# A token mixer's front on one core: query products ahead of the kv/value projection, the first projection in accumulator banks, two token mixes side by side

## The chip, the core and the metric

The kernel runs on one core of a Trainium2 chip. The metric is device time in microseconds (us), from a launch of the whole program: two layers for 384 tokens. TensorE (PE) does the matmuls and transposes, VectorE (DVE), ScalarE (ACT) and GpSimd (POOL) the elementwise work, and SyncE (SP) issues the DMAs that bring weights.

## The reference

Each layer is FFN 1, token mixer, FFN 2, all with a norm ahead and one behind. The tokens are 256 of a new stream (the prompt) and 8 × 16 of running streams with a cache (the sample). The widths are 1024 for the model, 8 heads with 64 + 32 columns, 384 for the query latent (cq), 256 for the kv latent, 256 for each of the other three branches. The mixer, to which the change belongs:

```python
def token_mixer(n, cos, sin, p, cache_lat, cache_kr, buf_b, buf_d):
    b, t, _ = n.shape
    h = n @ p['w_in']
    cq, ckv, kr, glu_in, uv, dproj, g = jnp.split(h, [O_Q, O_KV, O_KR, O_B, O_C, O_D], axis=-1)

    q = (rmsnorm(cq, p['q_norm']) @ p['w_uq']).reshape(b, t, A_HEADS, NOPE_DIM + ROPE_DIM)
    q_nope = q[..., :NOPE_DIM]
    q_rope = apply_rope(q[..., NOPE_DIM:], cos[:, None], sin[:, None])
    latent = rmsnorm(ckv, p['kv_norm'])
    k_rope = apply_rope(kr, cos, sin)
    if cache_lat is None:
        a = mla_prompt(q_nope, q_rope, latent, k_rope, p['w_ukv'])
    else:
        a = mla_sample(q_nope, q_rope,
                       jnp.concatenate([cache_lat.astype(latent.dtype), latent], axis=1),
                       jnp.concatenate([cache_kr.astype(k_rope.dtype), k_rope], axis=1),
                       p['w_ukv'])

    ga, gg = jnp.split(glu_in, 2, axis=-1)
    xb = ga * jax.nn.sigmoid(gg)
    bpad = jnp.concatenate([buf_b.astype(xb.dtype), xb], axis=1)
    yb = causal_dwconv(bpad, p['conv_b_w']) + p['conv_b_bias']
    yb = jax.nn.silu(layernorm(yb, p['conv_b_ln_g'], p['conv_b_ln_b']))
    new_b = bpad[:, -(CONV_B_WIDTH - 1):]

    u, v = jnp.split(uv, 2, axis=-1)
    v = layernorm(v, p['gmlp_vn_g'], p['gmlp_vn_b'])
    if cache_lat is None:
        yc = u * spatial_mix_prompt(v, p['gmlp_w_s'], p['gmlp_b_s'])
    else:
        yc = u * spatial_mix_sample(v, p['gmlp_w_s'], p['gmlp_b_s'])

    bg, cg, hd = jnp.split(dproj, 3, axis=-1)
    xd = cg * hd
    dpad = jnp.concatenate([buf_d.astype(xd.dtype), xd], axis=1)
    yd = bg * causal_dwconv(dpad, p['conv_d_w'])
    new_d = dpad[:, -(CONV_D_WIDTH - 1):]

    gates = jax.nn.sigmoid(g).reshape(b, t, N_BRANCH, D_MODEL)
    merged = (gates[:, :, 0] * (a @ p['w_br_a']) + gates[:, :, 1] * (yb @ p['w_br_b'])
              + gates[:, :, 2] * (yc @ p['w_br_c']) + gates[:, :, 3] * (yd @ p['w_br_d']))
    return merged @ p['w_o'], (latent, k_rope, new_b, v, new_d)
```

## The kernel before

The 384 tokens lie in three tiles t = 0, 1, 2 of 128; the third is the sample. Products are in fp32r, each as three: high × high, low × high, high × low (`mm3`, L313). For a weight the high part `wh` is a cast on ACT and the low part `wl` a subtraction on DVE (`split_unit`, L246); for the normalized activations `xh` and `xl` are made likewise, out of an accumulator bank into which PE has transposed them (`chain`, L397: `flip` L431 transposes and casts, `low` L441 subtracts). All instructions are recorded by one helper, so each row of the profile says L74, and the names tell them apart.

PSUM has eight banks. Six are accumulators, `acc(t,h)` for tile t and half h (L340); `bank()` (L336) goes round the six. Two rotate (`rot`, L344).

Weights come in units, in an order that `plan_mixer` (L562) writes down. In the front of the mixer these are: four units mA (the columns for cq and the rotated key kr, 416 wide, two of eight k-rows each), two units for conv(0), four units mB (kv latent and gMLP values, 512 wide), three units uq (query products: one for the rotated part, two for the rest), two units for conv(1), two units ukv, and so on. SP loads each unit to one of four stage buffers (`load_unit`, L225), then ACT and DVE split it.

The order of instructions on each engine is fixed when the program is built. `Core` is a planner: it keeps a clock of its own, costs each instruction, holds follow-up work as generators (`spawn`, `step`, L147 to L187) and takes up the one that is due; `take` and `drop` (L163, L174) say when a bank is free. Where it thinks DVE idle, it puts a tap of the long convolution there (`tap` L699, tile yTb; 62 a layer).

In `mixer_front` (L646) the work goes: for each tile the mA product by `heads` (L376), that is, sixteen matmuls on xh and, last, eight on xl; behind each, `latent_q` (L867) takes statistics (ACT's junk), rotates the key (kr), scales cq (half) and transposes it; then conv(0); then the mB product for each tile, followed by `latent_kv` and `gmlp_v` (L901, L926); then the query products, `rotate` (L955; three tiles, each evicted as four pieces of 32 partitions, by ACT and DVE in turn) and `nope` (L984; four); then conv(1). Later `dense` (L837) hands out the projections and token mixes that fill PE during the attention: short(0), short(1), mix(0), short_gate(0), mix(1), short_gate(1) and on. The piece of `heads` on which the first step rests:

```python
                mm(o, lhsT=self.xh[:, k, tt], rhs=wh, start=(k == 0), stop=False)
                mm(o, lhsT=self.xh[:, k, tt], rhs=wl, start=False, stop=False)
...
            self.need(("xL", t))
            for k in range(KD):
                if not first:
                    mm(o, lhsT=self.xl[:, k, tt], rhs=w(k)[0], start=False, stop=(k == KD - 1))
```

Of the kernel before, what the change touches and what calls it, by code (L numbers as in the profile page):

```python
# [8 lines left out]
F32 = mybir.dt.float32  # L9
# [3 lines left out]
ALU = mybir.AluOpType  # L13
# [3 lines left out]
P = 128  # L17
D = 1024
KD = D // P
T = 384  # L20
NT = 3
DFF = 2816
NC_FF = DFF // P
EPS = 1e-6
# [9 lines left out]
KL = 256  # L34
# [14 lines left out]
PE, ACT, DVE, POOL = "tensor", "scalar", "vector", "gpsimd"  # L49
# [50 lines left out]
class Core:  # L100
# [461 lines left out]
    def plan_mixer(self, units, l):  # L562
        a = self.a
        def fm(cs):
            for c in cs:
                units.append((("fm", l, c), a["in_f"][l, c], [KD, P], "M"))

        for h in range(4):
            units.append((("mA", l, h), a["in_a"][l, :, 2 * h:2 * h + 2, :], [2, 416], "M"))
        fm(range(0, 2))  # L570
        for h in range(4):
            units.append((("mB", l, h), a["in_b"][l, :, 2 * h:2 * h + 2, :], [2, 512], "M"))
        for h in range(3):
            units.append((("uq", l, h), a["w_uq"][l, h], [3, 256], "M"))
        fm(range(2, 4))
        for h in range(2):
            units.append((("ukv", l, h), a["w_ukv"][l, h], [2, 512], "M"))
        fm(range(4, 12))
        gate = lambda c, g: units.append((("g", l, c, g), a["in_g"][l, c, g], [KD, P], "M"))
        br = lambda c, h: units.append((("br", l, c, h), a["w_br"][l, c, :, 6 * h:6 + 4 * h, :], [6 - 2 * h, P], "M"))  # L580
        for g in range(4):
            gate(0, g)
        br(0, 0)
        br(0, 1)
        for c in range(1, KD):
            gate(c, 0)
            br(c, 0)
            for g in range(1, 4):
                gate(c, g)
            br(c, 1)  # L590
        for h in range(2):
            for k in range(4):
                units.append((("wo", l, h, k), a["w_o"][l, h, :, 2 * k:2 * k + 2, :], [2, 512], "M"))
# [52 lines left out]
    def mixer_front(self, l, m, mf, ma, aT, yT):  # L646
# [59 lines left out]
        def conv(c):  # L706
            xg = yield from project(2 * c)
            sg = mf.tile([P, T], F32, tag="t15", name="sg", bufs=2)
            self.spawn(("conv",), sigmoid(xg, sg), "rot")
            xa = yield from project(2 * c + 1)  # L710
            self.spawn(("conv",), conv_glu(c, xa, sg), "rot")
            yield
# [122 lines left out]
            yield from self.gate(l, 0, g, self.th[0, g])  # L835

        def dense():  # L837
            for f, c in ((short, 0), (short, 1), (mix, 0), (short_gate, 0), (mix, 1), (short_gate, 1), (mix_gate, 0), (mix_gate, 1),
                         (gate, 0), (gate, 1), (gate, 2)):
                yield from f(c)  # L840

# [2 lines left out]
        def run(gen):  # L844
            for _ in gen:
                pass

        with pool("mixq") as mq:
# [9 lines left out]
            keys = [("mA", l, h) for h in range(4)]  # L858

            def main(t):  # L860
                pas[t] = self.rot([416])
                return pas[t], lambda k: [w[:, k % 2, :] for w in self.weights(keys[k // 2])]

            def mid(t):
                self.spawn(("cq",), latent_q(t), "rot")

            def latent_q(t):  # L867
                tt = slice(t * P, (t + 1) * P)
# [16 lines left out]
                yield POOL  # L885
                cqn = self.half()
                nc.vector.scalar_tensor_tensor(cqn[:, :QL], pa[:, :QL], r, g_q, op0=ALU.mult, op1=ALU.mult)
                self.drop("rot")
                yield DVE
                tp = self.acc(t, 0)  # L890
                for j in range(3):
# [5 lines left out]

            self.heads(keys, main, mid)
            run(conv(0))

            def latent_kv(t, pb):  # L901
                tt = slice(t * P, (t + 1) * P)
                yield PE

                s, v, r = self.rms_stats(pb[:, :KL], "kv")
                yield ACT
                nc.vector.tensor_scalar(v, s, 1.0 / KL, EPS, op0=ALU.mult, op1=ALU.add)
                yield DVE
                self.power(r, v)
                yield POOL  # L910
                lat = lat_s if t == 2 else self.half()[:, :KL]
                nc.vector.scalar_tensor_tensor(lat, pb[:, :KL], r, g_kv, op0=ALU.mult, op1=ALU.mult)
                nc.sync.dma_start(out=a["o_lat"][l, tt, :], in_=lat)
                self.drop("acc")
                yield DVE
                tp = self.acc(t, 0)
                for j in range(2):
                    nc.tensor.transpose(tp[:, j * P:(j + 1) * P], lat[:, j * P:(j + 1) * P], self.ident)
                yield PE
                t2 = tp[:, :KL].rearrange("p (a b) -> p a b", a=2)  # L920
                if t < 2:
                    yield from self.split_into(lth[:, :, tt], ltl[:, :, tt], t2)
                else:
                    nc.scalar.copy(latTs, t2)

            def gmlp_v(t, pb):  # L926

                yield PE
                sv = self.small.tile([P, 10], F32, tag="sv", name="sv")
                nc.vector.bn_stats(sv[:, 0:6], pb[:, KL:])  # L930
                nc.vector.bn_aggr(sv[:, 6:8], sv[:, 0:6])
                v, r = sv[:, 8:9], sv[:, 9:10]
                nc.vector.tensor_scalar(v, sv[:, 7:8], EPS, None, op0=ALU.add)
                nc.vector.scalar_tensor_tensor(vn[t], pb[:, KL:], sv[:, 6:7], vn_g, op0=ALU.subtract, op1=ALU.mult)
                yield DVE
                self.power(r, v)
                yield POOL
                nc.vector.scalar_tensor_tensor(vn[t], vn[t], r, vn_b, op0=ALU.mult, op1=ALU.add)
                if t == 2:
                    nc.sync.dma_start(out=a["o_vc"][l], in_=vn[t])  # L940

            for t in range(NT):
                tt = slice(t * P, (t + 1) * P)
                pb = self.acc(t, 1)
                for k in range(KD):
                    w = self.weights(("mB", l, k // 2))
                    self.mm3(pb, (self.xh[:, k, tt], self.xl[:, k, tt]),
                             (w[0][:, k % 2, :], w[1][:, k % 2, :]), k == 0, k == KD - 1)
                    if t == NT - 1 and k % 2:
                        self.done(("mB", l, k // 2))  # L950
                self.spawn(("lat",), latent_kv(t, pb), "acc")
                self.spawn(("vn",), gmlp_v(t, pb), "acc")


            def rotate(t, o):  # L955
# [44 lines left out]
            for j in range(4):  # L1000
                w = self.weights(("uq", l, 1 + j // 2))
                o = self.bank()[:, :T]
                for k in range(3):
                    sl = slice(j % 2 * P, j % 2 * P + P)
                    self.mm3(o, (w[0][:, k, sl], w[1][:, k, sl]), (cqh[:, k, :], cql[:, k, :]), k == 0, k == 2)
                self.spawn(("q",), nope(j, o), "acc")
                if j % 2:
                    self.done(("uq", l, 1 + j // 2))
            run(conv(1))
            self.need(("lat",))  # L1010

# [524 lines left out]
```

## Time and profile before

| what | value |
|---|---|
| median of 3 runs | 1859.82 us (1858.51 to 1859.93) |
| the profiled execution | 1858.79 us, of it the span 1857.0 |
| PE busy | 1831.8 us, 99%, 10060 matmuls and transposes |
| weight loads of PE | 1704.4 us, 92% (beside the matmuls) |
| DVE / ACT / POOL busy | 952.6 / 699.7 / 47.7 us |
| mean granted clock of PE | 0.998 of full |

The span is the time from the first to the last instruction. A row of the timeline gives the start, the time of the instruction (of all, where several alike follow each other), the engine, output and inputs, and in brackets how long the engine stood idle before it and for whom it waited. Matmuls overlap, so the step from one start to the next is what one costs.

### The profile page before, as it was taken

Reading aid. Unit: us, or ns where it says so; the run is one execution under the profiler, and the core shown is the slowest. Engines: PE = TensorE matmul, PEld = TensorE weight load, DVE = VectorE, ACT = ScalarE, POOL = GpSimd, SP = SyncE. Lnnn points to the kernel's source line nnn. Section 1 sums busy time; section 2 is a strip of 40 time slices with the busy share of each in tenths; the row PEclk is TensorE's granted clock in tenths of the full one; section 3 lists DMA queues with packets and bytes.
Section 4 is the critical chain, followed back from the end, with each engine's and each line's share of the span. In section 5 each row is a group of like instructions: output and inputs, shape, how many; then the busy total and the mean of one; then the engine's idle time right before and its main releaser. Section 6 shows DMA issues by size and latency. Waiting matters only on the chain.

```text
span 1857.0 us, 25073 instructions
## 1 busy us (share of the span) xinstructions
PE 1831.8 (99%) x10060; PEld 1704.4 (92%) x10060; DVE 952.6 (51%) x1466; ACT 699.7 (38%) x1156; POOL 47.7 (3%) x96
## 2 busy tenths in 40 slices
PE   8999999999999999999999999999999999999998
PEld 6999998889999889999989999988899998999997
DVE  5333347896544463333463333478864446533333
ACT  5333334444333443333343333445343335333332
POOL 0000001000000000000000000010000000000000
PEclk9999999999999999999999999999999999999999
DMA  7444443452343443344444434344523434443441
GB/s 252 137 125 125 125 146 94 142 178 83 114 137 124 146 159 125 125 126 126 134 137 126 128 130 129 117 102 139 173 73 127 142 123 136 148 127 126 133 125 46
DMA packets 98087, 241.88 MB, mean 130 GB/s; under 512 B 28977, under 2 KB 39985, under 8 KB 97970
## 3 DMA queue, kind: packets, MB, share of 16 engines
q1 hardware_dynamic: 97826, 240.21, 41.4%
q8 instruction: 79, 1.29, 0.3%
q14 instruction: 38, 0.31, 0.1%
q10 hardware_dynamic: 144, 0.07, 0.0%
HBM read 236.63 MB, written 3.31 MB: 129 GB/s over the span
## 4 chain that ended last, share of the span: by engine, by line
PE 93%; DVE 4%; ACT 1%; issue 1%; POOL 0%; DMA 0%; POOLq 0%; DVEq 0%; ACTq 0%
PE rot L74 59%; PE acc L74 34%; DVE yTb L74 1%; DVE wl L74 1%; DVE half L74 1%; ACT wh L74 0%; ACT junk L74 0%; DVE sv L74 0%; DVE yTd L74 0%; DVE qTp L74 0%; DVE qa L74 0%; DVE xl L74 0%; DMA st<-in_f 0%; POOL ln L74 0%; POOL kv L74 0%
## 5 line engine op out<-in xcount | busy, mean ns | idle before, releaser
L74 DVE TENSOR_TENSOR wl<-st,wh 128x1024 fp32r<-128x1024 f32 (+3 forms) x426 | 500.1, 1185 | 479.3 <-ACT wh L74 468.3
L74 ACT CAST wh<-st 128x1024 fp32r<-128x1024 f32 (+3 forms) x426 | 428.5, 1018 | 665.1 <-issue 366.3
L74 PE MATMUL rot<-xh,wh 128*128 128x384 f32 x1984 | 669.1, 337 | 0.7 <-ACT sg L74 0.7
L74 PE MATMUL rot<-xh,wl 128*128 128x384 f32 x1984 | 665.7, 336 | 0.6 <-DVE wl L74 0.6
L74 PE MATMUL rot<-xl,wh 128*128 128x384 f32 x1984 | 665.1, 335 | 0.0
L74 PEld LDWEIGHTS rot<-xh,wh 128*128 128x128 f32 x1984 | 372.5, 188 | 8.0 <-issue 3.2
L74 PEld LDWEIGHTS rot<-xh,wl 128*128 128x128 f32 x1984 | 372.6, 188 | 5.0 <-DVE wl L74 1.0
L74 PEld LDWEIGHTS rot<-xl,wh 128*128 128x128 f32 x1984 | 372.5, 188 | 0.3 <-issue 0.3
L74 PE MATMUL acc<-wl,hh 128*128 128x512 f32 x528 | 207.2, 392 | 0.0
L74 PE MATMUL acc<-wh,hl 128*128 128x512 f32 x528 | 207.1, 392 | 0.0
L74 PE MATMUL acc<-wh,hh 128*128 128x512 f32 x528 | 205.4, 389 | 0.0
L74 DVE TENSOR_TENSOR hf<-sg,rot 128x384 f32<-128x384 f32 x80 | 44.4, 555 | 146.0 <-PE rot L74 146.0
L74 PEld LDWEIGHTS acc<-wl,hh 128*128 128x128 f32 x528 | 99.1, 188 | 20.8
L74 PEld LDWEIGHTS acc<-wh,hl 128*128 128x128 f32 x528 | 99.1, 188 | 19.1
L74 PEld LDWEIGHTS acc<-wh,hh 128*128 128x128 f32 x528 | 99.2, 188 | 18.9
L74 ACT ACTIVATE half<-rot 128x384 f32<-128x384 f32 x58 | 28.5, 492 | 167.2 <-PE rot L74 167.2
L74 DVE SCALAR_TENSOR_TENSOR half<-half,acc 128x384 f32<-128x384 f32 x44 | 24.4, 554 | 124.1 <-PE acc L74 124.1
L74 DVE SCALAR_TENSOR_TENSOR yTb<-bs,cols,yTb 128x384 f32<-128x384 f32 x120 | 73.8, 615 | 2.1
L74 PE MATMUL rot<-wl,xh 128*128 128x512 f32 (+1 forms) x144 | 55.7, 387 | 1.6 <-DVE wl L74 1.6
L74 PE MATMUL rot<-wh,xh 128*128 128x512 f32 (+1 forms) x144 | 56.3, 391 | 0.0
L74 PE MATMUL acc<-ident,half 128*128 128x128 f32 x262 | 43.9, 283 | 6.7 <-DVE half L74 5.4
L74 POOL TENSOR_TENSOR post<-post,neghalf 128x1 f32<-128x1 f32 x18 | 12.2, 679 | 1440.2 <-DVE post L74 1440.0
(221 smaller groups left out, 1631.7 us busy)
## 6 DMA issues: line engine op xcount, KB each, us to landing
st<-ffn_gp SPq DMA_DIRECT2D x160, 512.0 KB, 3.5
st<-ffn_dn SPq DMA_DIRECT2D x88, 512.0 KB, 3.5
st<-in_g SPq DMA_DIRECT2D x64, 512.0 KB, 3.7
st<-in_f SPq DMA_DIRECT2D x24, 512.0 KB, 4.0
st<-ffn_gs SPq DMA_DIRECT2D x16, 512.0 KB, 4.8
st<-w_o SPq DMA_DIRECT2D x16, 512.0 KB, 4.2
st<-w_br SPq DMA_DIRECT2D x16, 384.0 KB, 3.1
st<-in_b SPq DMA_DIRECT2D x8, 512.0 KB, 4.9
```

The costliest lines, as they stand in the source:

```text
L74: r = f(*args, **kw)
```

## The change

In `plan_mixer` the three uq units go ahead of the four mB units. The mA product of tile t goes to `acc(t,1)` instead of a rotating bank, and what follows it gives back an accumulator. The two functions behind the mB product, and the mB loop itself, move behind the query products without a change in them. In `dense` mix(1) goes ahead of short_gate(0). Nothing else changes.

```diff
--- before.py
+++ after.py
@@ -568,10 +568,10 @@
         for h in range(4):
             units.append((("mA", l, h), a["in_a"][l, :, 2 * h:2 * h + 2, :], [2, 416], "M"))
         fm(range(0, 2))
+        for h in range(3):
+            units.append((("uq", l, h), a["w_uq"][l, h], [3, 256], "M"))
         for h in range(4):
             units.append((("mB", l, h), a["in_b"][l, :, 2 * h:2 * h + 2, :], [2, 512], "M"))
-        for h in range(3):
-            units.append((("uq", l, h), a["w_uq"][l, h], [3, 256], "M"))
         fm(range(2, 4))
         for h in range(2):
             units.append((("ukv", l, h), a["w_ukv"][l, h], [2, 512], "M"))
@@ -835,7 +835,7 @@
             yield from self.gate(l, 0, g, self.th[0, g])
 
         def dense():
-            for f, c in ((short, 0), (short, 1), (mix, 0), (short_gate, 0), (mix, 1), (short_gate, 1), (mix_gate, 0), (mix_gate, 1),
+            for f, c in ((short, 0), (short, 1), (mix, 0), (mix, 1), (short_gate, 0), (short_gate, 1), (mix_gate, 0), (mix_gate, 1),
                          (gate, 0), (gate, 1), (gate, 2)):
                 yield from f(c)
 
@@ -858,11 +858,11 @@
             keys = [("mA", l, h) for h in range(4)]
 
             def main(t):
-                pas[t] = self.rot([416])
+                pas[t] = self.acc(t, 1)[:, :416]
                 return pas[t], lambda k: [w[:, k % 2, :] for w in self.weights(keys[k // 2])]
 
             def mid(t):
-                self.spawn(("cq",), latent_q(t), "rot")
+                self.spawn(("cq",), latent_q(t), "acc")
 
             def latent_q(t):
                 tt = slice(t * P, (t + 1) * P)
@@ -885,7 +885,7 @@
                 yield POOL
                 cqn = self.half()
                 nc.vector.scalar_tensor_tensor(cqn[:, :QL], pa[:, :QL], r, g_q, op0=ALU.mult, op1=ALU.mult)
-                self.drop("rot")
+                self.drop("acc")
                 yield DVE
                 tp = self.acc(t, 0)
                 for j in range(3):
@@ -897,59 +897,6 @@
 
             self.heads(keys, main, mid)
             run(conv(0))
-
-            def latent_kv(t, pb):
...
-            for t in range(NT):
-                tt = slice(t * P, (t + 1) * P)
-                pb = self.acc(t, 1)
-                for k in range(KD):
-                    w = self.weights(("mB", l, k // 2))
-                    self.mm3(pb, (self.xh[:, k, tt], self.xl[:, k, tt]),
-                             (w[0][:, k % 2, :], w[1][:, k % 2, :]), k == 0, k == KD - 1)
-                    if t == NT - 1 and k % 2:
-                        self.done(("mB", l, k // 2))
-                self.spawn(("lat",), latent_kv(t, pb), "acc")
-                self.spawn(("vn",), gmlp_v(t, pb), "acc")
...
@@ -1006,6 +953,60 @@
                 self.spawn(("q",), nope(j, o), "acc")
                 if j % 2:
                     self.done(("uq", l, 1 + j // 2))
+
+            def latent_kv(t, pb):
+                tt = slice(t * P, (t + 1) * P)
+                yield PE
...
+            for t in range(NT):
+                tt = slice(t * P, (t + 1) * P)
+                pb = self.acc(t, 1)
+                for k in range(KD):
+                    w = self.weights(("mB", l, k // 2))
+                    self.mm3(pb, (self.xh[:, k, tt], self.xl[:, k, tt]),
+                             (w[0][:, k % 2, :], w[1][:, k % 2, :]), k == 0, k == KD - 1)
+                    if t == NT - 1 and k % 2:
+                        self.done(("mB", l, k // 2))
+                self.spawn(("lat",), latent_kv(t, pb), "acc")
+                self.spawn(("vn",), gmlp_v(t, pb), "acc")
+
             run(conv(1))
             self.need(("lat",))
 
```

On PE in layer 0, the start of the mA product of the third tile, before (`xh_110`, `wh_2191`: high parts of x and of the first mA unit; `xl_111` the low part; `ident` marks transposes; in brackets the engines whose signals are waited for):

```order
L74 MATMUL acc_2547<-ident_106,half_2443 128x128 [waits DVE_49]
L74 MATMUL acc_2547<-ident_106,half_2443 128x128 x3
L74 MATMUL rot_2492<-wh_2252,xl_111 128x416
L74 MATMUL rot_2555<-wh_2191,xh_110 128x416 [waits Activation_49]
L74 MATMUL rot_2555<-wl_2192,xh_110 128x416
L74 MATMUL rot_2555<-wh_2191,xh_110 128x416
```

and with the change:

```order
L74 MATMUL acc_2547<-ident_106,half_2443 128x128 [waits DVE_49]
L74 MATMUL acc_2547<-ident_106,half_2443 128x128 x3
L74 MATMUL acc_2492<-wh_2252,xl_111 128x416
L74 MATMUL acc_2567<-wh_2191,xh_110 128x416 [waits DVE_49,PE_49,Activation_49]
L74 MATMUL acc_2567<-wl_2192,xh_110 128x416
L74 MATMUL acc_2567<-wh_2191,xh_110 128x416
```

The first matmul of the tile waited for ACT's cast alone, and now waits for DVE as well.

On DVE in layer 1, the four low parts of mB (`wl_10482`, `wl_10511`, `wl_10539`, `wl_10560`) before; `sg`, `bs` and `yTb` belong to conv(0) and the taps, `krT` and `cql` to the third tile's key and cq:

```order
L74 TENSOR_TENSOR wl_10482<-st_10086,wh_10481 128x1024
L74 COPY krT_10258<-acc_10502 32x128
L74 TENSOR_TENSOR wl_10511<-st_10110,wh_10510 128x1024
L74 TENSOR_TENSOR cql_10274<-acc_10502,cqh_10273 128x3x128
L74 TENSOR_SCALAR sg_10507<-sg_10507 128x384
L74 TENSOR_TENSOR wl_10539<-st_10450,wh_10538 128x1024
L74 TENSOR_TENSOR bs_10261<-rot_10508,sg_10507 128x24x16
L74 TENSOR_TENSOR wl_10560<-st_10479,wh_10559 128x1024
L74 TENSOR_SCALAR yTb_10242<-bs_10261,cols_8797 128x384
L74 SCALAR_TENSOR_TENSOR yTb_10242<-bs_10261,cols_8797,yTb_10242 128x384 x3
```

and with the change (`qTp`, `qr0`: evictions of query products; the second, third and fourth of the mB units are `wl_10653`, `wl_10684` and `wl_10703`; the first stands ahead of the rows shown):

```order
L74 TENSOR_SCALAR qTp_10277<-acc_10601 64x256
L74 TENSOR_SCALAR qr0_10256<-acc_10636 32x2x8x16 x2
L74 TENSOR_SCALAR qTp_10277<-acc_10630 64x256
L74 TENSOR_SCALAR yTb_10242<-bs_10261,cols_8797 128x384
L74 SCALAR_TENSOR_TENSOR yTb_10242<-bs_10261,cols_8797,yTb_10242 128x384
L74 TENSOR_TENSOR wl_10653<-st_10493,wh_10652 128x1024
L74 TENSOR_SCALAR qTp_10277<-acc_10650 64x256
L74 TENSOR_SCALAR qTp_10277<-acc_10671 64x256
L74 SCALAR_TENSOR_TENSOR yTb_10242<-bs_10261,cols_8797,yTb_10242 128x384
L74 TENSOR_TENSOR wl_10684<-st_10520,wh_10683 128x1024
L74 SCALAR_TENSOR_TENSOR yTb_10242<-bs_10261,cols_8797,yTb_10242 128x384
L74 TENSOR_TENSOR wl_10703<-st_10542,wh_10702 128x1024
```

The weights that stood among the work of conv(0) now stand behind evictions of the query products.

## Rows read from the trace of the kernel before

**Rows 1.** The page: engines, chain of waits, two groups on DVE (busy, mean ns).

```profile
PE 1831.8 (99%) x10060; PEld 1704.4 (92%) x10060; DVE 952.6 (51%) x1466; ACT 699.7 (38%) x1156; POOL 47.7 (3%) x96
...
PE 93%; DVE 4%; ACT 1%; issue 1%; POOL 0%; DMA 0%; POOLq 0%; DVEq 0%; ACTq 0%
...
L74 DVE TENSOR_TENSOR wl<-st,wh 128x1024 fp32r<-128x1024 f32 (+3 forms) x426 | 500.1, 1185 | 479.3 <-ACT wh L74 468.3
...
L74 DVE SCALAR_TENSOR_TENSOR yTb<-bs,cols,yTb 128x384 f32<-128x384 f32 x120 | 73.8, 615 | 2.1
```

**Rows 2.** PE's timeline, layer 0, first projection and conv(0): start, us, instruction, idle before.

```profile
291.48 0.35 PE L74 MATMUL rot<-wh,xh 128*128 128x416 f32 x1
...
296.89 0.35 PE L74 MATMUL rot<-wh,xh 128*128 128x416 f32 x1
...
303.18 0.46 PE L74 MATMUL rot<-wh,xh 128*128 128x416 f32 x1
...
307.44 0.55 PE L74 MATMUL acc<-ident,half 128*128 128x128 f32 x3 [0.60 <-DVE half L74]
...
314.48 0.41 PE L74 MATMUL rot<-xh,wh 128*128 128x384 f32 x1 [0.66 <-ACT sg L74]
```

**Rows 3.** DVE's timeline beside it.

```profile
290.33 1.28 DVE L74 TENSOR_TENSOR xl<-acc,xh 128x512 fp32r<-128x512 f32 x2
...
297.38 1.28 DVE L74 TENSOR_TENSOR xl<-acc,xh 128x512 fp32r<-128x512 f32 x2
...
304.27 0.35 DVE L74 TENSOR_TENSOR kr<-rot,rope_t 128x32 f32<-128x32 f32 x3 [1.18 <-ACT junk L74]
...
304.77 1.28 DVE L74 TENSOR_TENSOR xl<-acc,xh 128x512 fp32r<-128x512 f32 x2
```

**Rows 4.** ACT's timeline beside it.

```profile
302.54 1.22 ACT L74 CAST xh<-acc 128x512 fp32r<-128x512 f32 x2 [0.34 <-PE acc L74]
```

**Rows 5.** PE's timeline, layer 1, first projection and conv(0).

```profile
1221.21 0.46 PE L74 MATMUL rot<-wh,xh 128*128 128x416 f32 x1
...
1228.51 0.44 PE L74 MATMUL rot<-xh,wl 128*128 128x384 f32 x1 [0.65 <-DVE wl L74]
```

**Rows 6.** DVE's timeline, layer 1, the third tile's low part.

```profile
1222.80 1.28 DVE L74 TENSOR_TENSOR xl<-acc,xh 128x512 fp32r<-128x512 f32 x2
```

**Rows 7.** Busy time by window: both layers' kv/value and query products, then two stretches.

```profile
core 0: us, PE busy (x) PEld busy (x) DVE busy (x) ACT busy (x) POOL busy (x), PEclk, DMA share, GB/s
319.59:351.90 32.31, 29.54 (x149) 25.27 (x148) 26.33 (x62) 10.65 (x25) 3.68 (x6) 0.95 0.47 133
1237.64:1268.73 31.09, 28.28 (x148) 23.84 (x148) 25.14 (x59) 10.15 (x24) 3.71 (x6) 1.00 0.49 132
345.00:348.60 3.60, 3.16 (x12) 3.09 (x13) 2.79 (x5) 1.22 (x5) 0.00 (x0) 0.53 0.64 199
1262.00:1266.00 4.00, 2.48 (x17) 2.20 (x16) 3.09 (x6) 1.04 (x4) 0.00 (x0) 1.00 0.10 34
```

**Rows 8.** PE's timeline: start of kv/values in layer 0, the longest waits of both layers.

```profile
319.59 0.39 PE L74 MATMUL acc<-wh,xh 128*128 128x512 f32 x1
...
319.81 0.40 PE L74 MATMUL acc<-wh,xl 128*128 128x512 f32 x1
...
345.44 0.66 PE L74 MATMUL acc<-ident,lat_s 128*128 128x128 f32 x2 [1.57 <-DVE qTp L74]
...
1264.09 0.41 PE L74 MATMUL acc<-ident,lat_s 128*128 128x128 f32 x2 [1.52 <-DVE qTp L74]
```

**Rows 9.** DVE's timeline: evictions of the query products, layers 0 and 1.

```profile
344.87 0.43 DVE L74 TENSOR_SCALAR qTp<-acc 32x256 f32<-32x256 f32 x1 [0.44 <-ACT qTp L74]
...
1262.66 0.42 DVE L74 TENSOR_SCALAR qTp<-acc 32x256 f32<-32x256 f32 x1
...
1263.51 0.43 DVE L74 TENSOR_SCALAR qTp<-acc 32x256 f32<-32x256 f32 x1 [0.44 <-ACT qTp L74]
...
1273.40 0.43 DVE L74 TENSOR_SCALAR qTp<-acc 64x256 f32<-64x256 f32 x1 [0.42 <-ACT qTp L74]
```

**Rows 10.** DVE's timeline, layer 0: the bias behind mix(0).

```profile
401.37 0.62 DVE L74 TENSOR_TENSOR yTc<-rot,gbias 128x256 f32<-128x256 f32 x2
```

More of the change, by code (lines that the diff above doesn't have):

```diff
@@ L899, in mixer_front @@
             run(conv(0))
-            def latent_kv(t, pb):
-                tt = slice(t * P, (t + 1) * P)
[L903 to L940, printed above, removed]
@@ L942, in mixer_front @@
-            for t in range(NT):
-                tt = slice(t * P, (t + 1) * P)
-                pb = self.acc(t, 1)
-                for k in range(KD):
-                    w = self.weights(("mB", l, k // 2))
-                    self.mm3(pb, (self.xh[:, k, tt], self.xl[:, k, tt]),
-                             (w[0][:, k % 2, :], w[1][:, k % 2, :]), k == 0, k == KD - 1)
-                    if t == NT - 1 and k % 2:
-                        self.done(("mB", l, k // 2))
-                self.spawn(("lat",), latent_kv(t, pb), "acc")
-                self.spawn(("vn",), gmlp_v(t, pb), "acc")
@@ L1008, in mixer_front @@
                     self.done(("uq", l, 1 + j // 2))
+            def latent_kv(t, pb):
+                tt = slice(t * P, (t + 1) * P)
+                yield PE
+                s, v, r = self.rms_stats(pb[:, :KL], "kv")
+                yield ACT
+                nc.vector.tensor_scalar(v, s, 1.0 / KL, EPS, op0=ALU.mult, op1=ALU.add)
+                yield DVE
+                self.power(r, v)
+                yield POOL
+                lat = lat_s if t == 2 else self.half()[:, :KL]
+                nc.vector.scalar_tensor_tensor(lat, pb[:, :KL], r, g_kv, op0=ALU.mult, op1=ALU.mult)
+                nc.sync.dma_start(out=a["o_lat"][l, tt, :], in_=lat)
+                self.drop("acc")
+                yield DVE
+                tp = self.acc(t, 0)
+                for j in range(2):
+                    nc.tensor.transpose(tp[:, j * P:(j + 1) * P], lat[:, j * P:(j + 1) * P], self.ident)
+                yield PE
+                t2 = tp[:, :KL].rearrange("p (a b) -> p a b", a=2)
+                if t < 2:
+                    yield from self.split_into(lth[:, :, tt], ltl[:, :, tt], t2)
+                else:
+                    nc.scalar.copy(latTs, t2)
@@ new lines, in gmlp_v @@
+            def gmlp_v(t, pb):
+                yield PE
+                sv = self.small.tile([P, 10], F32, tag="sv", name="sv")
+                nc.vector.bn_stats(sv[:, 0:6], pb[:, KL:])
+                nc.vector.bn_aggr(sv[:, 6:8], sv[:, 0:6])
+                v, r = sv[:, 8:9], sv[:, 9:10]
+                nc.vector.tensor_scalar(v, sv[:, 7:8], EPS, None, op0=ALU.add)
+                nc.vector.scalar_tensor_tensor(vn[t], pb[:, KL:], sv[:, 6:7], vn_g, op0=ALU.subtract, op1=ALU.mult)
+                yield DVE
+                self.power(r, v)
+                yield POOL
+                nc.vector.scalar_tensor_tensor(vn[t], vn[t], r, vn_b, op0=ALU.mult, op1=ALU.add)
+                if t == 2:
+                    nc.sync.dma_start(out=a["o_vc"][l], in_=vn[t])
```

## The prediction, made before the changed kernel had run

> **What bounds the kernel now.** I read the page from the top. The busy times come first: TensorE (PE) works 1831.8 of 1857.0 us, 99%, and the chain that ended last is 93% PE [rows 1]. So only PE's standing time can be won or lost, some 25 us in all, and a change that keeps PE's instructions (10060 matmuls before; the changed one issues the same ones, in another order and to other banks) moves the time by what PE waits, to the microsecond. The second thing to see is who ends those waits: DVE is busy only half of the span (51%), but its commonest work, the low parts of the weights (wl, 426 times 1.19 us), is done one at a time, in the order in which the program lists it, between evictions and convolution taps [rows 1]. Third I read PE's rows through the front of the mixer in both layers, because every edit lies there. In a free run a 512-column matmul follows the last after 0.23 us [rows 8], so by columns one of 384 after 0.17. From the first kv/value matmul to the first of conv(1) PE takes 32.31 us in layer 0, of it 29.54 busy, and 31.09 in layer 1, 28.28 busy [rows 7]. Both layers wait 2.8 us there; the longest wait is 1.57 or 1.52 us for the evictions of the query products (qTp) [rows 8].
>
> The sum below goes against the profiled execution: 1858.79 us, span 1857.0, 1.8 around it. The median of the three runs is 1859.82, 0.06% higher; less than 0.2% (3.7 us) I don't count as a difference.
>
> **First part: the first projection goes to an accumulator bank.** Before, the product for token tile t went to one of two rotating banks, and its first matmul waited for the cast of x's high part (xh, ACT) alone. Now it goes to the bank acc(t,1), out of which, just before, ACT casts xh and DVE takes the low part xl. The order fence on PE shows the new wait on DVE. The matmul needs no xl for its first sixteen instructions, but it now needs xl's bank. Behind it on PE, nothing can pass.
> - Tile 0: xl ends at 290.33+1.28 = 291.61, PE was there at 291.48 [rows 2, 3]: 0.1, and 0.1 more from the release to the start, as behind the qTp that ended at 344.87+0.43 = 345.30, when PE began at 345.44 [rows 8, 9]. Some 0.2.
> - Tile 1: xl ends at 297.38+1.28 = 298.66, PE was there at 296.89 [rows 2, 3]: 1.8, less the 0.2 by which PE is late already, 1.6. The xl itself doesn't move; it hangs on the FFN's end.
> - Tile 2: xl stands on DVE behind the rotated key (kr) of tile 1, and that waited for ACT's square of tile 1's product (junk), which begins when tile 1's product and the cast xh (302.54+1.22) are done [rows 3, 4]. All this moves with PE, by 1.8: xl ends at 304.77+1.28+1.8 = 307.9; PE arrives at 303.18+1.8 = 305.0. It waits 2.9.
>
> Together 4.7. Layer 1 has the same three within 0.2; at its third tile PE is there at 1221.21 and xl ends at 1222.80+1.28 = 1224.08, both later by 1.8 [rows 5, 6]. 4.8 in all. What goes: PE's wait of 0.60 for the normalized cq of tile 1 at 307.44, since cq is older by then, about 1.0 if the restart counts too (an estimate) [rows 2]. The 0.66 at 314.48 for a rotating bank (sg) also goes, but the transposes of tile 2's cq, which come out of the later product, then wait about 0.75; layer 1's wait for wl at 1228.51, 0.65, stays [rows 2, 5]. So the next phase begins 3.5 us late in layer 0 and 3.4 in layer 1. Ends: nothing, if xl can be early enough each time, and 4.7 per layer, if nothing is given back. I take 3.5 and 3.4, as walked through row by row.
>
> **Second part: query products ahead of kv and values.** The instructions are the same. Work without waits is 32.31 − 2.8 = 29.5 in layer 0, which includes a clock drop (below) of some 1.4, and 28.3 in layer 1, so about 28.2 for both. The moved loads are the same seven DMAs in another order on SP; no other queue is passed, and their landing is far enough ahead. What changes is what DVE and ACT must do, and when. The query evictions are a chain: in layer 1 they run from 1262.66 to 1273.83, 11.2 us with two wl of 1.2 between them, so 8.8 us by themselves, since ACT and DVE take turns at a bank (DVE waits 0.44 for ACT's share) [rows 9]. Before, that chain ran beside the last query products and conv(1), which needs two weight units and no more, and PE waited only 1.5 for it. Now it stands right ahead of the kv/value products, whose first token tile uses up four new units in 24 × 0.23 = 5.5 us. Each needs a wl of 1.2 (and a cast of 1.0 on ACT). The second fence shows it: in layer 1 three of the four wl stand behind the evictions, with taps of 0.61 each put between.
> - Layer 1: DVE has from the first eviction to the wl of the last unit 8.8 + 3 × 1.2 + about 4 taps × 0.61 = 14.8 us. PE has until then four query products (36 matmuls × 0.17 = 6.2) and three quarters of the first tile (4.1), 10.3. The 4.5 between them is what PE waits for weights. Walked through instruction by instruction, with the casts that stand behind ACT's share of the evictions, it is 5.0 (1.8, 0.8, 2.1 and 0.3 at the four units). The transposes of the latents, whose chain stands behind taps, add 0.9: 6 in all.
> - Layer 0: two of the four wl come ahead of the chain, so 8.8 + 2.4 + 2.4 = 13.6 against 10.3, 3.3. The walk has it as 0.5 at a query transpose, 1.2 for the bank of the third rotation's eviction, 0.3 and 1.3 at weights. Latent transposes add 1.3: 4.6.
>
> So layer 0 takes 28.2 + 4.6 = 32.8 instead of 32.3, layer 1 28.2 + 6 = 34.2 instead of 31.1: +0.5 and +3.1. Ends: all these waits gone, −4.1 and −2.8, or the chain in full view, 3 more in each layer.
>
> The evictions' turns can be looked at with the Trainium skill, "PSUM — Partial Sum Buffer", Terms, where a quadrant is 32 consecutive partitions and two engines may use different quadrants of one bank at the same time. The trace shows DVE's qTp of one quadrant waiting 0.44 us for ACT's of another [rows 9], so here the program's own waits make them take turns; by the rule, without these waits, each bank would come free 0.4 us sooner, 1.3 a layer, and the sum would be some 2.6 less. No edit removes those waits, and I keep the row.
>
> **The clock.** In layer 0 the granted clock is 0.53 from 345.00 to 348.60, about the lower of the two levels (1.2 of 2.4 GHz), right after PE's wait of 1.57. In layer 1 the like wait of 1.52 was followed by 1.00 [rows 7, 8]. The drop costs 1.6 at most (half of 3.16 busy) and 1.2 by the difference of the two phases; I use 1.4. The new waits of 2.9 and 2.1 may bring it. From one drop in two such waits I put half of it into each layer: 1.4 in all.
>
> **Third part: the two mixes side by side.** mix(1) now follows mix(0) at once, on the other rotating bank, and short_gate(0) takes the bank that mix(0) leaves. That bank is free when DVE has added the bias (yTc, from 401.37, 0.62) [rows 10]; the projection wants it some 2.5 us later (counted in matmuls of the order). So hidden; if DVE were busy with taps then, 0.6 to 1.2 a layer. I take +0.2 for both layers, ends −1 and +2.
>
> **The sum.** 3.5 + 3.4 + 0.5 + 3.1 + 0.2 = 10.7, and 1.4 for the clock: 12.1. Nothing later takes it back, since PE has no slack: 1858.8 + 12.1 = 1870.9. Part of the waits of the second part is my walk's, which can count a wait twice; I say 1870.
>
> **Rivals.**
> 1. Only the accumulator bank costs; the new waits of the second part are no longer than the old ones and the clock stays. 6.9 + 0 + 0.2, and 1.4 less for layer 0's drop: 1858.8 + 5.7 = 1864.5. For it: layer 0 has two of its wl early. Against: the places of the wl in layer 1.
> 2. The clock drops in both layers, twice in one of them, and the latent transposes wait in full: 10.7 + 3 × 1.4 + 2 = 16.9 above, 1875.7. For it: waits nearly twice as long as the one that was followed by the drop. Against: layer 1's 1.52 had none.
> 3. Not slower: the query products, which need nothing but cq and three small units, fill the time in which kv's weights are made, and the old waits of that phase go without a successor: −2.8 twice, −1.4 for the clock, against +6.9: 1858.8 − 0.1 = 1858.7, no change. Place: from 319.59 and 1237.64 on. It decides if the seven weights' wl are done before the first qTp. For it: this is where PE now waits longest. Against: one DVE row list, in which three of them stand behind it.
> 4. Faster: as 3, and xl of tile 2 comes sooner than I have it, because DVE is free ahead of kr, so that the bank costs 1.8 a layer instead of 3.5: 1855.3. Against: DVE's kr row, which waits for ACT and has xl behind it.
>
> **How the numbers follow.** Forecast 0.55, rival 1 0.17, rival 2 0.13, rival 3 0.10, rival 4 0.05. The forecast's own range is 1866 to 1874. Slower by over 0.2% (above some 1863): forecast, and rivals 1 and 2, 0.85. Same: rival 3, 0.10. Faster: 0.05. The range from 1861 to 1877 leaves out rivals 3 and 4 and little above.
>
> **What would show it.** Right: the 416-column matmuls of tiles 1 and 2 begin after a PE wait on xl of about 1.6 and 2.9 us in both layers; waits on wl in the first kv/value tile of layer 1; conv(1) 4 us late in layer 0 and 6 in layer 1, with whatever the clock adds; behind it the two profiles run in step. Wrong: no PE wait on xl (then the bank was free sooner than the walk says), a kv/value tile without waits, or a difference that arises later than the mixer's front.

## The result, and the profile after

The changed kernel took 1871.66 us (median of 6 runs, 1871.61 to 1873.05), the kernel before 1858.55 beside it: a ratio of 1.0070, interval 1.0057 to 1.0083, or 13.1 us slower. The forecast was 1870. The profiled execution took 1871.61 us, its span is 1869.8, 12.8 longer than before.

The page of the changed kernel first, engines and chain, against [rows 1]:

```profile
PE 1834.6 (98%) x10060; PEld 1705.7 (91%) x10060; DVE 951.9 (51%) x1466; ACT 700.9 (37%) x1156; POOL 46.6 (2%) x96
...
PE 92%; DVE 6%; ACT 1%; issue 1%; POOL 0%; DMA 0%; POOLq 0%; SPq 0%; DVEq 0%; ACTq 0%
```

PE does the same 10060 instructions and is busy 2.8 us longer over the whole program; the rest of the 12.8 is standing time. So the question is where PE stands and where it runs slower. I matched equal matmuls of both traces and took the shift of their starts. PE's timeline of the changed kernel, the rows that answer to [rows 2, 5, 8]:

```profile
291.71 0.46 PE L74 MATMUL acc<-wh,xh 128*128 128x416 f32 x1
...
298.76 0.45 PE L74 MATMUL acc<-wh,xh 128*128 128x416 f32 x1 [1.38 <-DVE xl L74]
...
308.16 0.69 PE L74 MATMUL acc<-wh,xh 128*128 128x416 f32 x1 [2.87 <-DVE cq L74]
...
321.02 0.55 PE L74 MATMUL acc<-ident,half 128*128 128x128 f32 x3 [0.65 <-DVE half L74]
...
1223.57 0.46 PE L74 MATMUL acc<-wh,xh 128*128 128x416 f32 x1 [1.36 <-DVE xl L74]
...
1232.99 0.69 PE L74 MATMUL acc<-wh,xh 128*128 128x416 f32 x1 [2.87 <-DVE cq L74]
```

The last matmul of the FFN is 0.05 us late. Then come the waits of the first part: 1.38 ahead of tile 1 and 2.87 ahead of tile 2, in layer 1 1.36 and 2.87. (The profile names cq as releaser of the 2.87, a tiny instruction that ends with xl.) DVE's timeline beside it shows the chain as it was read in [rows 3]: kr waits 1.18 for ACT's square, and xl stands behind it and ends at 308.01; PE starts at 308.16.

```profile
306.24 0.35 DVE L74 TENSOR_TENSOR kr<-acc,rope_t 128x32 f32<-128x32 f32 x3 [1.18 <-ACT junk L74]
...
306.73 1.28 DVE L74 TENSOR_TENSOR xl<-acc,xh 128x512 fp32r<-128x512 f32 x2
```

How much of the first part is standing and how much is clock can be read from busy time by stretch, from the first 416-column matmul to the end of conv(0). Kernel before:

```profile
core 0: us, PE busy (x) PEld busy (x) DVE busy (x) ACT busy (x) POOL busy (x), PEclk, DMA share, GB/s
291.48:319.59 28.11, 26.85 (x153) 24.67 (x152) 19.45 (x45) 12.75 (x25) 4.17 (x6) 1.00 0.43 106
1209.51:1237.64 28.13, 26.88 (x152) 24.64 (x151) 20.60 (x46) 12.67 (x25) 4.17 (x6) 1.00 0.42 107
```

and the changed kernel, with a short stretch behind each 2.87 us wait, and last the stretches from conv(0) to conv(1):

```profile
core 0: us, PE busy (x) PEld busy (x) DVE busy (x) ACT busy (x) POOL busy (x), PEclk, DMA share, GB/s
291.60:326.45 34.85, 29.93 (x152) 26.96 (x152) 19.76 (x46) 12.23 (x25) 3.92 (x6) 0.90 0.38 95
1216.50:1249.58 33.08, 28.49 (x151) 25.98 (x152) 19.69 (x45) 13.19 (x26) 3.27 (x6) 0.95 0.38 100
308.00:314.40 6.40, 6.24 (x19) 5.29 (x20) 0.69 (x3) 0.15 (x1) 0.55 (x1) 0.51 0.00 0
1232.90:1236.00 3.10, 3.01 (x9) 2.91 (x10) 0.62 (x2) 0.00 (x0) 0.55 (x1) 0.52 0.02 5
326.45:358.46 32.01, 28.34 (x147) 23.56 (x146) 27.21 (x59) 12.77 (x28) 2.61 (x4) 1.00 0.38 99
1249.58:1282.61 33.03, 29.16 (x146) 23.33 (x146) 27.44 (x59) 12.75 (x28) 2.62 (x4) 1.00 0.35 104
```

Standing time (length less PE busy) went from 1.26 to 4.92 us in layer 0 and from 1.25 to 4.59 in layer 1: 3.7 and 3.3 more. The forecast had 3.5 and 3.4. Busy time for the same instructions went up by 3.1 and 1.6: that is the granted clock, 0.51 and 0.52 behind the long wait in both layers. The low clock of the kernel before, at 345 us [rows 7], is gone, and with it 1.4 us: the kernel with the mixes alone (experiment 1) does the same work in that phase with the same waits, had a clock of 1.00 there, and took 30.89 us for what took 32.31.

```profile
core 0: us, PE busy (x) PEld busy (x) DVE busy (x) ACT busy (x) POOL busy (x), PEclk, DMA share, GB/s
319.66:350.55 30.89, 28.12 (x148) 23.88 (x148) 25.94 (x61) 9.49 (x24) 3.67 (x6) 1.00 0.48 139
```

Between conv(0) and conv(1), that is from 326.45 to 358.46 and from 1249.58 to 1282.61, the phase takes 32.0 and 33.0 us, against 32.3 and 31.1 [rows 7]. With a clock of 1.00 on both sides that is 1.1 and 1.9 us more. The longest of its waits now, in the kv/value products:

```profile
338.83 0.47 PE L74 MATMUL acc<-wh,xh 128*128 128x512 f32 x1 [1.19 <-DVE qr L74]
...
344.67 0.50 PE L74 MATMUL acc<-wl,xh 128*128 128x512 f32 x1 [0.99 <-DVE wl L74]
...
349.94 0.44 PE L74 MATMUL acc<-ident,half 128*128 128x128 f32 x2 [0.88 <-DVE half L74]
...
1263.87 0.50 PE L74 MATMUL acc<-wl,xh 128*128 128x512 f32 x1 [1.48 <-DVE wl L74]
...
1265.45 0.50 PE L74 MATMUL acc<-wh,xh 128*128 128x512 f32 x1 [0.37 <-ACT wh L74]
...
1267.84 0.50 PE L74 MATMUL acc<-wl,xh 128*128 128x512 f32 x1 [1.67 <-DVE wl L74]
...
1274.12 0.44 PE L74 MATMUL acc<-ident,half 128*128 128x128 f32 x2 [0.22 <-DVE half L74]
```

Layer 0 waits for the eviction of the rotated queries (qr), for one wl and for the latents; layer 1 three times for weights (twice for wl on DVE, once for a cast on ACT), as the order of DVE's instructions had it. Shift by stretch:

| stretch | layer 0 | layer 1 |
|---|---|---|
| first projection and conv(0), standing | +3.7 | +3.3 |
| the same, slower clock and starts | +3.1 | +1.8 |
| query, kv and value products | −0.3 | +1.9 |
| from conv(1) on | +0.2 | −1.0 |

With the 0.05 at the start these make 12.8.

### The profile page after: what moved, and what is told of

The parts are those of the page before. It is cut to its first block, busy times and chain, and to the rows that moved or that the text cites. A ratio compares the mean times of both kernels' runs of the same rounds, so it can differ in the third digit from the quotient of the medians.

```text
span 1869.8 us, 25082 instructions
## 1 busy us (share of the span) xinstructions
PE 1834.6 (98%) x10060; PEld 1705.7 (91%) x10060; DVE 951.9 (51%) x1466; ACT 700.9 (37%) x1156; POOL 46.6 (2%) x96
## 4 chain that ended last, share of the span: by engine, by line
PE 92%; DVE 6%; ACT 1%; issue 1%; POOL 0%; DMA 0%; POOLq 0%; SPq 0%; DVEq 0%; ACTq 0%
PE rot L74 58%; PE acc L74 34%; DVE yTb L74 2%; DVE half L74 1%; DVE wl L74 1%; DVE xl L74 0%; ACT junk L74 0%; DVE x L74 0%; ACT wh L74 0%; DMA ck<-krT 0%; DVE yTd L74 0%; DVE qTp L74 0%; DVE qa L74 0%; DVE yTc L74 0%; DVE sx L74 0%
## 5 line engine op out<-in xcount | busy, mean ns | idle before, releaser
L74 PEld LDWEIGHTS acc<-ident,half 128*128 128x128 f32 x262 | 33.6, 145 | 17.4 <-DVE half L74 7.7
L74 PE MATMUL acc<-wh,xh 128*128 128x416 f32 (+1 forms) x96 | 39.2, 408 | 10.1 <-DVE cq L74 5.7
```

Source lines behind the costliest of these rows:

```text
L74: r = f(*args, **kw)
```

## The experiments

Each time is a median, with the ratio to the kernel before on the same chip and its interval.

**1. One part at a time.** Only the accumulator bank (what follows the product gives back an accumulator, as in the change):

```diff
-                pas[t] = self.rot([416])
+                pas[t] = self.acc(t, 1)[:, :416]
...
```

> The kernel before with one part of the change: the first projection accumulates in acc(t,1); order of query products, kv/values and mixes as before. Theory (the wait for the low part xl in the same bank, and the clock that falls behind the longest of these waits, make nearly all of the loss): PE waits about 1.4 and 2.9 us ahead of tiles 1 and 2 in both layers, the granted clock is near 0.5 behind the second, and the time is 9 to 12 us above before. Rival A (the bank wait is taken back later, the loss belongs to the new order of query and kv products): under 4 us above before.

1868.87 us against 1858.57, ratio 1.0049 (1.0037 to 1.0062). The profile has the same waits and the low clock behind them:

```profile
298.69 0.46 PE L74 MATMUL acc<-wh,xh 128*128 128x416 f32 x1 [1.38 <-DVE xl L74]
...
308.11 0.68 PE L74 MATMUL acc<-wh,xh 128*128 128x416 f32 x1 [2.87 <-DVE cq L74]
```

```profile
core 0: us, PE busy (x) PEld busy (x) DVE busy (x) ACT busy (x) POOL busy (x), PEclk, DMA share, GB/s
308.00:311.00 3.00, 2.89 (x8) 2.80 (x9) 0.64 (x2) 0.00 (x0) 0.55 (x1) 0.50 0.00 0
1232.60:1236.00 3.40, 3.40 (x13) 3.14 (x12) 0.41 (x1) 0.00 (x0) 0.00 (x0) 0.51 0.02 5
```

Rival A falls: this part alone is 10.3 of the 13.1. One of its five runs had a mean granted clock of 0.999, and that one took 1865.39; the others had 0.996 or 0.997 and took 1868.1 to 1869.0. So, by that one run, the standing time alone is about 6.8 us, what the forecast gave the bank, and the clock the other 3.

Only the query products first, in code and in the order of the weights (the diff of the change without its other edits):

> The kernel before with one part of the change: query products ahead of the kv/value projection, in code and in the order of the weights; first projection in rotating banks, mixes as before. Theory: the phase from conv(0) to conv(1) takes what it took in the changed kernel, 32.0 and 33.0 us instead of 32.3 and 31.1, so 0 to 3 us above before. Rival A (the loss belongs to this order): 6 to 10 us above before.

1860.76 us, 1.0009 (1.0000 to 1.0017): 2.2 us. The theory's range held; the phase is no place of a large loss.

Only the two mixes side by side:

```diff
-            for f, c in ((short, 0), (short, 1), (mix, 0), (short_gate, 0), (mix, 1), (short_gate, 1), (mix_gate, 0), (mix_gate, 1),
+            for f, c in ((short, 0), (short, 1), (mix, 0), (mix, 1), (short_gate, 0), (short_gate, 1), (mix_gate, 0), (mix_gate, 1),
```

> The kernel before with one part of the change: the two token mixes side by side. Theory: hidden, within 1 us of before. Rival (the projection behind the mixes waits for the bias on DVE): 1 to 3 us above before.

1861.16 us, 1.0013 (1.0004 to 1.0022): 2.6 us. The same program measured again (experiment 5, second run) was 1.5 us above before, and the single runs of both with a mean granted clock of 0.999 took 1859.64 and 1859.66, some 1 us above; so part of either median is clock. My theory (hidden) fell all the same, and the rival's time came by another mechanism. PE's timeline with the mixes side by side, and then before, where the sample's first transposes wait for pn:

```profile
408.70 0.41 PE L74 MATMUL acc<-ident,half 128*128 128x128 f32 x2 [1.11 <-DVE pn L74]
```

```profile
408.13 0.44 PE L74 MATMUL rot<-wst,vn 128*64 128x128 f32 x4
...
409.05 0.41 PE L74 MATMUL acc<-ident,half 128*128 128x128 f32 x2 [0.48 <-DVE pn L74]
```

Before, mix(1) began at 408.13, between the projection and these transposes; it covered part of the wait for the softmax (pn). Side by side it ran ahead, and PE waits 1.11 instead of 0.48. No projection waits for the bias.

**2. Taking the bank's wait away.** The first attempt put tile t into another accumulator:

```diff
-                pas[t] = self.acc(t, 1)[:, :416]
+                pas[t] = self.acc((t + 2) % 3, 1)[:, :416]
```

> The changed kernel, with the first projection of tile t in acc((t+2) mod 3, 1), a bank whose own xl is done or not yet due, instead of acc(t,1). All else as in the changed kernel. Theory: the waits of 1.4 and 2.9 us ahead of tiles 1 and 2 go, the granted clock stays at 1.00 there, and the time is that of query-products-first and mixes together, 0 to 3 us above before. Rival B (accumulators as such cost, since latent_q holds them longer and others go round the six): 1866 or more. Rival C (DVE's kr waits later anyway, so that the time comes back at the transposes of cq): 1865 to 1868.

1875.24 us, 1.0087 (1.0074 to 1.0101), slower than the change itself. All three expectations missed what happened: tile 0 now went to acc(2,1), which held the last tile of the FFN until DVE had taken it out.

```profile
296.91 0.69 PE L74 MATMUL acc<-wh,xh 128*128 128x416 f32 x1 [5.24 <-DVE half L74]
```

The waits of tiles 1 and 2 were gone, but this 5.24 us took their place. The next attempt leaves tile 0 in a rotating bank:

```diff
-                pas[t] = self.acc(t, 1)[:, :416]
+                pas[t] = self.acc(t - 1, 1)[:, :416] if t else self.rot([416])
...
```

> The changed kernel, with the first projection of tile 0 in a rotating bank and that of tiles 1 and 2 in acc(t-1,1), the bank of the tile before, whose xl is done. The run before this had tile 0 in acc(2,1), which the last tile of the FFN still held: PE waited 5.2 us there in each layer, so that it tested another wait than it was meant to. Theory: no PE wait ahead of any first projection, granted clock 1.00 there, and the time of query-products-first plus mixes (2.2 and 2.6 us above before as measured alone): 3 to 6 us above before. Rival B (accumulators as such cost): 8 us or more above before. Rival C (the wait comes back at the transposes of cq): 7 to 10.

1859.66 us, 1.0008 (0.9999 to 1.0017). No wait ahead of any tile, clock 1.00:

```profile
core 0: us, PE busy (x) PEld busy (x) DVE busy (x) ACT busy (x) POOL busy (x), PEclk, DMA share, GB/s
291.00:420.00 129.00, 122.16 (x764) 108.92 (x763) 108.16 (x251) 59.08 (x142) 10.61 (x21) 1.00 0.52 149
1215.00:1370.00 155.00, 147.71 (x945) 130.31 (x945) 125.03 (x293) 68.30 (x158) 11.64 (x24) 1.00 0.43 125
```

12.0 of the 13.1 us are gone, by a bank whose xl is done. Accumulators as such cost nothing; the wait does. It came out below my 3 to 6. The two small parts do not simply add up, and the clock is one reason: this trace has a granted clock of 1.00 through both mixers' fronts, while query products first alone had 0.50 from 1255.8 us on, the mixes alone from 1264.7 on, and the kernel before from 345 on [rows 7].

**3. Why tile 2 waits longest.** kr computed one step later, so that xl stands ahead of it on DVE:

```diff
+                yield ACT
+                nc.vector.tensor_scalar(v, s, 1.0 / QL, EPS, op0=ALU.mult, op1=ALU.add)
+                yield DVE
                 nc.vector.tensor_tensor(kr[:, 0, :], pa[:, QL:QL + RD], cs, op=ALU.mult)
...
-                yield ACT
-                nc.vector.tensor_scalar(v, s, 1.0 / QL, EPS, op0=ALU.mult, op1=ALU.add)
-                yield DVE
```

> The changed kernel, with the rotated key kr of each tile computed one step later, so that on DVE the xl of tile 2 stands ahead of tile 1's kr. Theory: PE's wait ahead of tile 2 falls from 2.87 to about 1.8 us in both layers, since xl then follows ACT's cast and not the square behind it; with the low clock behind it shortened, 2 to 5 us below the changed kernel. Rival D (xl waits for the cast itself, kr's place is no cause): the wait stays within 0.3 us of 2.87.

1865.69 us, 1.0034 (1.0022 to 1.0047). On PE the wait fell to 0.84, further than I said:

```profile
306.11 0.46 PE L74 MATMUL acc<-wh,xh 128*128 128x416 f32 x1 [0.84 <-DVE xl L74]
```

because on DVE xl now follows ACT's cast at once, and starts at 304.73 instead of 306.73:

```profile
304.73 1.32 DVE L74 TENSOR_TENSOR xl<-acc,xh 128x512 fp32r<-128x512 f32 x2
```

In the profiled execution (1863.98 us) no low clock follows it, though PE now waits 3.29 at the first kv/value product; three of the five runs had a lower mean clock, 0.996 or 0.997, and took 1865.7 to 1867.2. The median is 6.0 below the change. Rival D falls: kr's place was the cause of the third wait's size.

**4. Taps among the weights.** Query products first alone, with taps held back from the first query product to the last kv/value product:

```diff
-            while self.idle and self.free[DVE] - self.now < 100:
+            while self.idle and not self.hold and self.free[DVE] - self.now < 100:
...
+            self.hold = True
...
+            self.hold = False
```

> Query-products-first alone (as run before), and no convolution tap is put on DVE from the first query product to the last kv/value product; they come later. Theory: in layer 1 PE's waits for wl in the first kv/value tile (0.82, 0.39 and 1.66 us) fall to 1 to 2 us in all, since taps stood among them; the waits of the latents' transposes (0.85 in layer 0, 0.46 in layer 1) go. 1 to 3 us below query-products-first. Rival E (the chain of evictions alone makes these waits): no more than 0.5 us below.

1857.84 us, 0.9998 (0.9990 to 1.0007), 2.9 below query products first (1.5 to 1.9 between runs with the same mean clock). In layer 1 the waits for weights are 0.44, 0.39 and 1.13 (1.96 in all, was 2.87), and the latents' transposes wait 0.21 in layer 0 (was 0.85). Rival E falls: one third of the wait for weights was taps. The other two thirds I put down to the chain of evictions; no run takes that chain away.

**5. Taps ahead of the softmax.** The same hold during the sample's attention, with the mixes side by side:

> The mixes side by side alone (as run before), and no convolution tap is put on DVE during the sample's attention; they come later. Side by side alone PE waited 1.11 us for pn in layer 0 (before 0.48) and 0.98 and 0.26 in layer 1: mix(1) no longer stands ahead of the transposes that need pn. Theory: pn is late because taps stand ahead of its chain on DVE; without them the waits go, 2 to 3 us below mixes side by side. Rival F (the chain of maximum, exponential and reciprocal is that long itself): the waits stay, within 0.7 us of mixes side by side.

1894.93 us, 1.0195 (1.0181 to 1.0209). DVE's timeline shows the maximum (sx) taken as soon as PE's scores are there, at 404.11, and pn ready at 405.66+0.23 = 405.89; PE waits for it nowhere:

```profile
404.11 0.44 DVE L74 TENSOR_REDUCE sx<-acc 128x1 f32<-128x272 f32 x1 [1.04 <-PE acc L74]
...
405.66 0.23 DVE L74 TENSOR_SCALAR pn<-half,sx 128x16 f32<-128x16 f32 x1
```

So far the theory holds, and rival F falls: the chain from the scores to pn takes 1.78 us when no tap stands in it. But the taps held back were left for the end. In layer 0, 26 of them start after 440 us (in the kernel before, the last tap starts at 428.49), sixteen in one row right ahead of the convolution's norm (the next text's 19 taps and 11.6 us twice are not what the trace has). DVE's row, and then PE's wait for it, 10.11 us in layer 0 and 11.65 in layer 1:

```profile
453.92 10.43 DVE L74 SCALAR_TENSOR_TENSOR yTb<-bs,cols,yTb 128x384 f32<-128x384 f32 x16
```

```profile
464.40 1.65 PE L74 MATMUL rot<-yTb,ones 128*128 128x384 f32 x2 [10.11 <-DVE yTb L74]
```

A shorter hold, from a half's last scores to the end of its softmax:

> The mixes side by side alone; taps are kept off DVE only from a half's last score matmuls to the end of its softmax, so that they end where they ended before (the run without taps in the whole sample attention pushed 19 of them in front of the convolution's norm, where PE then waited 11.6 us twice). Theory (pn is late because taps stand ahead of its chain): PE's waits for pn, 1.11 us in layer 0 and 0.98 and 0.26 in layer 1, fall under 0.3 in all, 1.5 to 3 us below mixes side by side. Rival F (the chain is that long itself): waits and time within 0.5 us of mixes side by side.

1860.59 us, 1.0008 (1.0000 to 1.0017), with the same waits for pn, 1.12, 0.98 and 0.26. That looks like rival F, but there was no hold at all: the edit sets `self.hold`, and the line that reads it, shown in experiment 4, is not in this kernel. The trace lists the same instructions in the same order as that of the mixes alone, on all four engines, with five taps (3.22 us) in front of sx and two more behind it.

```profile
403.25 3.22 DVE L74 SCALAR_TENSOR_TENSOR yTb<-bs,cols,yTb 128x384 f32<-128x384 f32 x5
...
406.38 0.43 DVE L74 TENSOR_REDUCE sx<-acc 128x1 f32<-128x272 f32 x1
...
408.38 0.23 DVE L74 TENSOR_SCALAR pn<-half,sx 128x16 f32<-128x16 f32 x1
```

So this run says nothing on F. It is a second measurement of the mixes alone, 1.5 us above before. That taps make pn late rests on the run before it and on the last one of experiment 6.

**6. Towards a faster version.** Three combinations:

> The kernel before (kv/values first, mixes apart), with the first projection of tiles 1 and 2 in the bank of the tile before, and taps kept off DVE from a half's last scores to the end of its softmax. Theory: the wait for a rotating bank (0.66 us in layer 0) and the waits for pn go, all else as before: 1 to 3 us below before. Rival: each wait removed shows another behind it, within 0.7 us of before.

1859.16 us against 1859.12, 0.9999 (0.9990 to 1.0008): nothing gained, and the waits for pn stayed (0.47, 0.36), since the hold is not read here either. What is left of the edit is the bank of the tile before, alone in the kernel before: it costs nothing, and rival B of experiment 2 falls by this run too.

> Query products first without taps among them (as run before), and the first projection of tiles 1 and 2 in the bank of the tile before. Theory: rotating banks cost nothing once their 0.66 us is replaced by the transposes' wait, so the same time as query-products-first without taps, within 1 us. Rival: accumulators save 2 us, as the run with both other parts of the change might be read.

1858.09 us, 0.9993 (0.9985 to 1.0002): as query products first without taps. The rival falls, accumulators save nothing.

> As the run before it in this list, and taps kept off DVE during the softmax of the sample's first half. Theory: the waits for pn of that half go (0.5 us in each layer), and the taps' end moves by one, without a wait at the convolution's norm: 0.5 to 2 us below that run, and 1 to 3 us below before. Rival: taps come too late again, and PE waits at the norm: above before.

1878.15 us, 1.0100 (1.0085 to 1.0116): the rival. In this kernel the hold is read. DVE takes sx as soon as the scores are there, and no wait for pn is left in either layer:

```profile
403.87 0.44 DVE L74 TENSOR_REDUCE sx<-acc 128x1 f32<-128x272 f32 x1 [0.45 <-PE acc L74]
```

But the last taps end after 456 us, and PE waits 2.58 (for taps), 1.98 and 2.38 at the norm in layer 0; the granted clock is 0.50 there, from 457.50 to 471.00. None of the twelve beats the kernel before clear of the noise.

## Why the prediction was right

**The accumulator bank.** The step that carried the forecast, and it held in its size: 0.2, 1.6 and 2.9 us were forecast for the three tiles and 0.2, 1.4 and 2.9 measured; 3.5 and 3.4 net, and 3.7 and 3.3 measured. Experiments 1, 2 and 3 show the cause, the xl in the same bank and kr ahead of it on DVE. Rival 4 (DVE is free ahead of kr) is refuted by the same rows.

**The clock.** The term that was mis-sized most. I put half a drop of 1.4 into each layer, for waits in either part: 1.4 in all. The trace has two drops, both behind the bank's 2.9, and in layer 0 the low clock lasted through 6.2 us of work: 3.1 and 1.6 us, 4.7 (4.9 with slower starts). The loss of the kernel before at 345 went, 1.4 as the next term had it.

**The new order of queries and values.** Over-sized: +0.5 and +3.1 forecast, −0.3 and +1.9 measured. In waits, 4.6 and 6.0 were forecast; PE stood 3.7 and 3.9 us, and with slower starts behind the waits layer 1 lost 4.8 (33.0 less 28.2). The mechanism is right (waits for qr, wl and latents, with taps among the weights). In layer 0 the walk had 0.5 at a transpose, 1.2 for qr, 1.6 for weights and 1.3 for latents, and 0.61, 1.19, 0.99 and 0.88 came. In layer 1 it gave the four weight units 5.0 where 3.5 came, and the latents 0.9 where 0.22 came. Alone the part costs 2.2 us. Rival 3 fell on the waits in layer 1, and rival 1 on the same waits, which are longer than the old 2.8 in both layers, and on the clock; of rival 2 only the size of the clock came (4.2 against 4.9, in two drops and not three).

**The mixes.** I took +0.2 for the bias and its bank. The bias is hidden, as said; what I left out is that mix(1) had been the cover of the softmax. Alone it costs 2.6 or 1.5 us in the two measurements, around my end of +2. In the changed kernel the stretch from conv(1) on is 0.8 shorter all the same: it waits 2.8 us for pn, where the kernel before waits 0.8, but 0.94 and 0.47 at the matmuls with dg, which the kernel before has, went. Why these went was not tested.

Nor did it hold that nothing later takes anything back. In layer 1 the lag of the changed kernel falls from 14.1 us (equal matmuls at 1289.30 and 1303.36) to 13.5 at transposes of the attention, for which the kernel before waits and the changed one, coming later, does not. PE's timeline before, and then with the change:

```profile
1293.01 0.82 PE L74 MATMUL acc<-ident,half 128*128 128x128 f32 x4 [0.43 <-DVE half L74]
```

```profile
1306.48 0.60 PE L74 MATMUL acc<-ident,half 128*128 128x128 f32 x4
```

So the totals, 12.1 and 12.8 in the profiled pair, lie closer than their terms: the bank right, the clock 3.5 too low, the new order 2.0 and the rest 1.0 too high. That the total came within 0.7 us is luck: the last three errors nearly cancel.

The page's rule on quadrants (Trainium skill, "PSUM — Partial Sum Buffer", Terms) moved no number: evictions still take turns with 0.44 us in the trace after.

```profile
1255.92 0.88 DVE L74 TENSOR_SCALAR qTp<-acc 32x256 f32<-32x256 f32 x2 [0.44 <-ACT qTp L74]
```

## What to carry to other kernels

A bank is free when its last reader is done, not when the data in it is no longer needed by the work that follows; before a product moves to another bank, look for whoever still reads there, and on that engine for what stands ahead of the reader. Where PE is 99% busy, a wait of 3 us can cost 3 more in the clock behind it. A piece of work that looks like a filler may be the cover of another chain, so ask what runs in its place once it is moved.

## What the runs showed of the hardware

A PE wait's length alone did not tell whether the clock falls behind it. Behind 2.87 us the granted clock was near 0.5 in both layers of the changed kernel and of experiment 1 with the bank alone; behind 3.29 us (experiment 3, the profiled execution) it was 1.00; behind 1.57 and 1.52 us the kernel before fell in layer 0 and not in layer 1 [rows 7, 8]. The mixes side by side have the same two waits and fell in layer 1, not in layer 0; the same program in its second measurement (experiment 5) fell behind neither. Busy time by stretch, behind the 3.29 of experiment 3:

```profile
core 0: us, PE busy (x) PEld busy (x) DVE busy (x) ACT busy (x) POOL busy (x), PEclk, DMA share, GB/s
335.14:339.00 3.86, 3.86 (x17) 3.22 (x18) 3.72 (x6) 1.43 (x3) 0.00 (x0) 1.00 0.48 128
```

and behind the 1.57 and the 1.52 of the mixes side by side (PEclk is the third column from the right), in the last row behind the 1.52 of the second measurement:

```profile
core 0: us, PE busy (x) PEld busy (x) DVE busy (x) ACT busy (x) POOL busy (x), PEclk, DMA share, GB/s
345.54:348.60 3.06, 3.06 (x19) 3.02 (x20) 2.38 (x4) 0.90 (x3) 0.00 (x0) 1.00 0.60 191
1264.66:1268.00 3.34, 3.34 (x12) 3.25 (x13) 2.13 (x4) 1.21 (x4) 0.00 (x0) 0.50 0.32 108
1264.33:1268.00 3.67, 3.67 (x24) 3.64 (x24) 2.22 (x4) 1.67 (x5) 0.00 (x0) 1.00 0.44 142
```

So what a new wait costs in clock was not to be worked out from the trace of before; only that it can.
